# A log-softmax on one core: a row on 4 partitions instead of 8, pieces shifted by their own maximum, stores issued from ScalarE

## The chip, the cores and the metric

Each kernel runs on one core of one Trainium2 chip. The three rounds of experiments ran on three different chips, each with runs of the kernel before beside them. The metric is the device time of one execution in microseconds (us). Every run here was of the fast state, with a granted clock of 1.0, so runs are compared as they are. A ratio is the mean time of one kernel's fast runs over that of the other's fast runs of the same rounds, so it isn't quite the ratio of the medians that are quoted.

## The reference

```python
x: float32 [16, 512, 50000]
shifted = x - max(x, axis=-1)
out = shifted - log(sum(exp(shifted), axis=-1))
```

8192 rows of 50,000 values, each read once and written once: 1638.4 MB each way.

## The kernel before

A row lies on 8 partitions, so a tile is 16 rows, 128 partitions of 6250 columns (25,000 B) and 3.2 MB. There are eight such buffers and 512 tiles. `front` takes the maximum, combines it over the 8 partitions, and sums the exponentials on ScalarE; `back` rewrites the tile in place and stores it. `back` of a tile runs after `front` of the next one. All transfers are issued by SyncE.

```python
G = 8; NBUF = 8; AHEAD = 5

def load(t):
    buf = data.tile([P, W], FP32, name="buf")
    nc.sync.dma_start(out=buf, in_=xt[t])
    ...
def back(t):
    buf = tiles.pop(t)
    nc.vector.tensor_scalar(out=buf, in0=buf, scalar1=shift.pop(t)[:, 0:1],
        scalar2=logs.pop(t), op0=ALU.add, op1=ALU.subtract)
    nc.sync.dma_start(out=ot[t], in_=buf)

for t in range(AHEAD):
    load(t)
for t in range(ntiles + 1):
    if t + AHEAD < ntiles:
        load(t + AHEAD)      # the buffer of tile t + AHEAD - 8
    if t < ntiles:
        front(t)
    if t >= 1:
        back(t - 1)
```

What matters later is the order on SyncE's queue: the load of tile t+5 comes first and waits until the store of tile t-3 has landed, since it takes that buffer; the store of tile t-1 comes behind it.

## Time and profile before

| | before |
|---|---|
| time, median (range) | 7904.87 us (7893.95 to 7924.88) |
| bytes moved, mean rate | 3276.8 MB, 414 GB/s |
| busy: VectorE, ScalarE, TensorE | 70%, 40%, 8% |
| DMA share | 99.9%, one queue |

The prediction shows the page's DMA rows, the chain and the groups. One more view was in the trace and I passed over it: a stretch of the timeline of the kernel before. Its columns are start in us, duration in us, engine, line, operation. "SPq" is SyncE's issuing of a transfer.

```profile
2996.76 3.49 DVE L117 TENSOR_SCALAR buf<-buf,negmax,logsum 128x6250 f32<-128x6250 f32 x1
...
3012.91 0.33 SPq L75 DMA_DIRECT2D buf<-in_x_dram  x1
3012.92 3.50 DVE L117 TENSOR_SCALAR buf<-buf,negmax,logsum 128x6250 f32<-128x6250 f32 x1
...
3013.29 0.43 SPq L121 DMA_DIRECT2D out_dram<-buf  x1
```

The first rewrite ended at 3000.25, yet its store is issued at 3013.29, right after the load at 3012.91. For 13 us a finished tile stood in its buffer because the load ahead of it on the queue was waiting.

### The profile page before, as it was taken

What the parts mean: (1) busy time and instruction counts of PE and PEld (TensorE: products, weight loads), DVE (VectorE), ACT (ScalarE), POOL (GpSimd) and SP (SyncE); (2) the same over time, 40 slices, a digit from 0 to 9 for tenths busy, and PEclk for the clock granted to TensorE, in tenths of its full rate; (3) what the DMA queues carried; (4) which work ended last, traced back from release to release, by engine and by line L of the source; (5) the groups of instructions that cost most, each with busy time, mean ns of one, the idle gap of its engine ahead of it and who ended that gap; (6) DMA issues with size and microseconds to landing.
All of it is one profiled execution on the core that took longest, in us unless ns stands there. A gap on an engine that the chain in (4) does not pass through costs nothing.

```text
span 7908.9 us, 12333 instructions
## 1 busy us (share of the span) xinstructions
PE 600.4 (8%) x2048; PEld 513.0 (6%) x2048; DVE 5566.8 (70%) x3072; ACT 3152.9 (40%) x2561; POOL 1.2 (0%) x7
## 2 busy tenths in 40 slices
PE   0000000000000000000000000000000000000000
PEld 0000000000000000000000000000000000000000
DVE  8777777777777776766666666766666666766665
ACT  4444444444444444333343434333343434333333
POOL 0000000000000000000000000000000000000000
DMA  9999999999999999999999999999999999999999
GB/s 416 426 430 431 431 431 431 431 431 431 431 430 431 429 428 410 410 403 409 409 406 403 404 405 408 407 408 405 409 408 401 406 403 413 408 405 406 406 405 385
DMA packets 147536, 3277.65 MB, mean 414 GB/s; under 512 B 16384, under 2 KB 16384, under 8 KB 16384
## 3 DMA queue, kind: packets, MB, share of 16 engines
q1 hardware_dynamic: 147456, 3276.87, 99.9%
q14 instruction: 64, 0.52, 0.0%
q8 instruction: 16, 0.26, 0.0%
HBM read 1638.40 MB, written 1638.40 MB: 414 GB/s over the span
## 4 chain that ended last, share of the span: by engine, by line
DMA 97%; SPq 1%; DVE 1%; issue 0%; ACT 0%; PE 0%; ACTq 0%
DMA out_dram<-buf 97%; SPq L75 1%; DVE pmax L81 1%; DMA buf<-in_x_dram 0%; DVE buf L117 0%; ACT dump L102 0%; DVE allmax L84 0%; DVE rowmax L86 0%; DVE spread L91 0%; DVE negmax L96 0%; PE rowsum L108 0%; ACT logsum L112 0%; ACTq L102 0%
## 5 line engine op out<-in xcount | busy, mean ns | idle before, releaser
L81 DVE TENSOR_REDUCE pmax<-buf 128x1 f32<-128x6250 f32 x512 | 3411.6, 6663 | 2231.9 <-DMA buf<-in_x_dram 2231.9
L102 ACT ACTIVATE dump<-buf,negmax 128x3125 f32<-128x3125 f32 x1024 | 2937.9, 2869 | 4370.9 <-DVE negmax L96 4354.4
L117 DVE TENSOR_SCALAR buf<-buf,negmax,logsum 128x6250 f32<-128x6250 f32 x512 | 1789.8, 3496 | 4.5 <-ACT logsum L112 3.6
L108 PE MATMUL rowsum<-part,ones 128*128 128x1 f32 x2048 | 600.4, 362 | 7269.8 <-ACT dump L102 7269.8
L108 PEld LDWEIGHTS rowsum<-part,ones 128*128 128x128 f32 x2048 | 513.0, 311 | 7357.1 <-ACT dump L102 7335.3
L112 ACT ACTIVATE logsum<-rowsum 128x1 f32<-128x1 f32 x512 | 87.8, 171 | 345.8 <-PE rowsum L108 345.8
L102 ACT ACTIVATION_READ_ACCUMULATOR dump<-buf,negmax 128x1 f32 x1024 | 190.8, 186 | 0.0
L96 DVE STREAM_TRANSPOSE negmax<-spread 128x32 f32<-128x32 f32 x512 | 108.2, 211 | 17.7
L84 DVE STREAM_TRANSPOSE allmax<-pmax 128x32 f32<-128x32 f32 x512 | 108.2, 211 | 17.5
L86 DVE TENSOR_REDUCE rowmax<-allmax 128x4 f32<-128x32 f32 x512 | 95.3, 186 | 17.8
L91 DVE COPY spread<-rowmax 128x32 f32<-128x32 f32 x512 | 92.9, 181 | 17.8
L67 ACT ACT_TABLE_LOAD x1 | 1.3, 1283 | 0.8 <-PEq L146 0.8
L59 POOL TENSOR_SCALAR_AFFINE_SELECT ones<-ones 128x128 f32<-128x128 f32 x1 | 0.4, 403 | 0.1
L63 POOL TENSOR_SCALAR_AFFINE_SELECT ones<-ones 128x128 f32<-128x128 f32 x1 | 0.4, 398 | 0.1
L57 POOL MEMSET ones<- 128x128 f32 x1 | 0.2, 204 | 0.3 <-POOLq L146 0.3
L146 POOL MEMSET const-bfloat16-1.0<- 128x1 bf16 x1 | 0.1, 102 | 0.0
L146 POOL MEMSET const-uint8-127<- 128x1 uint8 x1 | 0.1, 102 | 0.0
L146 POOL MEMSET const-float32-0.0<- 128x1 f32 x1 | 0.1, 99 | 0.3 <-issue 0.3
L146 POOL MEMSET const-float32-1.0<- 128x1 f32 x1 | 0.1, 99 | 0.0
## 6 DMA issues: line engine op xcount, KB each, us to landing
buf<-in_x_dram SPq DMA_DIRECT2D x512, 3125.0 KB, 23.5
out_dram<-buf SPq DMA_DIRECT2D x512, 3125.0 KB, 30.7
```

What stands on the lines that cost most here:

```text
L59: nc.gpsimd.affine_select(out=ones3, in_=ones3, pattern=[[-G, R], [0, G]], base=0, channel_multiplier=1, compare_op=ALU.is_ge, fill=0.0,)
L67: nc.scalar.preload_act_table_set("natural_log_exp_and_others")
L75: nc.sync.dma_start(out=buf, in_=xt[t])
L81: nc.vector.reduce_max(out=pmax, in_=buf, axis=AX)
L84: nc.vector.transpose(out=allmax, in_=pmax.to_broadcast([P, SQ]))
L86: nc.vector.tensor_reduce(out=rowmax, in_=allmax.rearrange("p (r g) -> p r g", g=G), op=ALU.max, axis=AX, negate=True,)
L91: nc.vector.tensor_copy(out=spread.rearrange("p (r g) -> p r g", g=G), in_=rowmax[:, :, None].to_broadcast([P, SQ // G, G]),)
L96: nc.vector.transpose(out=negmax, in_=spread)
L102: nc.scalar.activation(out=dump, in_=buf[:, j * EXP_C : (j + 1) * EXP_C], func=ACT.Exp, bias=negmax[:, 0:1], scale=1.0, accum_out=part[:, ...
L108: nc.tensor.matmul(rowsum, ones, part[:, j : j + 1], start=j == 0, stop=j == nexp - 1)
L112: nc.scalar.activation(out=logsum, in_=rowsum, func=ACT.Ln)
L117: nc.vector.tensor_scalar(out=buf, in0=buf, scalar1=shift.pop(t)[:, 0:1], scalar2=logs.pop(t), op0=ALU.add, op1=ALU.subtract,)
```

## The change

The intent is fewer, larger tiles: a row on 4 partitions gives 32 rows per tile, 6.4 MB, rows of 50,000 B, four buffers (the same 200,000 B per partition). So that a tile's latency stays short, each piece of 3125 columns is shifted by its own maximum, so that its exponential can run while VectorE reduces the next piece; the four sums are rescaled to the row's maximum at the end. A tile is finished before the next starts. Stores are issued from ScalarE, so they have a queue of their own. The diff, cut to its core:

```diff
-G = 8
+G = 4
-NBUF = 8
-AHEAD = 5
+NBUF = 4
...
-        nc.vector.reduce_max(out=pmax, in_=buf, axis=AX)
...
+        for j in range(nexp):
+            piece = buf[:, j * EXP_C : (j + 1) * EXP_C]
+            nc.vector.tensor_reduce(
+                out=negm[:, j : j + 1], in_=piece, op=ALU.max, axis=AX, negate=True
+            )
+            dump = dump_pool.tile([P, EXP_C], FP32, name="dump")
+            nc.scalar.activation(
+                out=dump, in_=piece, func=ACT.Exp,
+                bias=negm[:, j : j + 1], scale=1.0, accum_out=part[:, j : j + 1],
+            )
...
+        nc.scalar.activation(
+            out=scale, in_=negm, func=ACT.Exp, bias=negmax[:, 0:1], scale=-1.0
+        )
+        nc.vector.tensor_mul(out=scaled, in0=scale, in1=part)
...
-        nc.sync.dma_start(out=ot[t], in_=buf)
+        nc.scalar.dma_start(out=ot[t], in_=buf)
...
+    for t in range(ntiles):
+        compute(t)
+        if t + NBUF < ntiles:
+            load(t + NBUF)
```

More of the change, by code (lines that the diff above doesn't have):

```diff
@@ L69 @@
     tiles = {}
-    shift = {}
-    logs = {}
     def load(t):
@@ L76, in load, with compute @@
         tiles[t] = buf
-    def front(t):
-        buf = tiles[t]
-        pmax = stats.tile([P, 1], FP32, name="pmax")
-        nc.vector.reduce_max(out=pmax, in_=buf, axis=AX)
-        allmax = stats.tile([P, SQ], FP32, name="allmax")
-        nc.vector.transpose(out=allmax, in_=pmax.to_broadcast([P, SQ]))
-        rowmax = stats.tile([P, SQ // G], FP32, name="rowmax")
+    def compute(t):
+        buf = tiles.pop(t)
+        negm = stats.tile([P, nexp], FP32, name="negm")
+        part = stats.tile([P, nexp], FP32, name="part")
+        for j in range(nexp):
[8 more added lines that the diff above has]
+            )
+        negp = stats.tile([P, 1], FP32, name="negp")
+        nc.vector.tensor_reduce(out=negp, in_=negm, op=ALU.min, axis=AX)
+        allneg = stats.tile([P, SQ], FP32, name="allneg")
+        nc.vector.transpose(out=allneg, in_=negp.to_broadcast([P, SQ]))
+        rowneg = stats.tile([P, SQ // G], FP32, name="rowneg")
         nc.vector.tensor_reduce(
-            out=rowmax, in_=allmax.rearrange("p (r g) -> p r g", g=G),
-            op=ALU.max, axis=AX, negate=True,
+            out=rowneg, in_=allneg.rearrange("p (r g) -> p r g", g=G),
+            op=ALU.min, axis=AX,
         )
@@ L92, in front @@
             out=spread.rearrange("p (r g) -> p r g", g=G),
-            in_=rowmax[:, :, None].to_broadcast([P, SQ // G, G]),
+            in_=rowneg[:, :, None].to_broadcast([P, SQ // G, G]),
         )
@@ L96, in front @@
         nc.vector.transpose(out=negmax, in_=spread)
-        shift[t] = negmax
-        part = stats.tile([P, nexp], FP32, name="part")
-        for j in range(nexp):
-            dump = dump_pool.tile([P, EXP_C], FP32, name="dump")
-            nc.scalar.activation(
-                out=dump, in_=buf[:, j * EXP_C : (j + 1) * EXP_C], func=ACT.Exp,
-                bias=negmax[:, 0:1], scale=1.0, accum_out=part[:, j : j + 1],
-            )
+        scale = stats.tile([P, nexp], FP32, name="scale")
+        nc.scalar.activation(
+            out=scale, in_=negm, func=ACT.Exp, bias=negmax[:, 0:1], scale=-1.0
+        )
+        scaled = stats.tile([P, nexp], FP32, name="scaled")
+        nc.vector.tensor_mul(out=scaled, in0=scale, in1=part)
         rowsum = sum_pool.tile([P, 1], FP32, name="rowsum")
@@ L108, in front @@
             nc.tensor.matmul(
-                rowsum, ones, part[:, j : j + 1], start=j == 0, stop=j == nexp - 1
+                rowsum, ones, scaled[:, j : j + 1], start=j == 0, stop=j == nexp - 1
             )
@@ L112, in front @@
         nc.scalar.activation(out=logsum, in_=rowsum, func=ACT.Ln)
-        logs[t] = logsum
-    def back(t):
-        buf = tiles.pop(t)
         nc.vector.tensor_scalar(
-            out=buf, in0=buf, scalar1=shift.pop(t)[:, 0:1], scalar2=logs.pop(t),
+            out=buf, in0=buf, scalar1=negmax[:, 0:1], scalar2=logsum,
             op0=ALU.add, op1=ALU.subtract,
         )
-        nc.sync.dma_start(out=ot[t], in_=buf)
-    for t in range(AHEAD):
+        nc.scalar.dma_start(out=ot[t], in_=buf)
+    for t in range(min(NBUF, ntiles)):
         load(t)
-    for t in range(ntiles + 1):
-        if t + AHEAD < ntiles:
-            load(t + AHEAD)
-        if t < ntiles:
-            front(t)
-        if t >= 1:
-            back(t - 1)
+    for t in range(ntiles):
+        compute(t)
+        if t + NBUF < ntiles:
+            load(t + NBUF)
 _INS = ['x']
```

## The prediction

> **What bounds the kernel now.** I read the page from its DMA rows first, then the chain of waits, then the DMA queue's own waits, then VectorE's groups. The page says this of the transfers and of the chain:
>
> ```profile
> DMA  9999999999999999999999999999999999999999
> GB/s 416 426 430 431 431 431 431 431 431 431 431 430 431 429 428 410 410 403 409 409 406 403 404 405 408 407 408 405 409 408 401 406 403 413 408 405 406 406 405 385
> DMA packets 147536, 3277.65 MB, mean 414 GB/s; under 512 B 16384, under 2 KB 16384, under 8 KB 16384
> q1 hardware_dynamic: 147456, 3276.87, 99.9%
> ...
> HBM read 1638.40 MB, written 1638.40 MB: 414 GB/s over the span
> ...
> DMA 97%; SPq 1%; DVE 1%; issue 0%; ACT 0%; PE 0%; ACTq 0%
> ```
>
> The reader is to see two things. The 16 DMA engines have work all the time (99.9%), on one queue, and the chain that ended last is 97% DMA: the time is bytes over rate, 3276.8 MB at 414 GB/s = 7915 us against a span of 7908.9. And the rate has two regimes: 431 GB/s until about 2.9 ms, then about 406 to the end. A view of the windows 600 to 2600 us and 3000 to 7000 us gives 431 and 407 GB/s at a DMA share of 1.00 in both, so the second regime isn't a lack of queued transfers; the same packets take longer. Per engine 431/16 = 26.94 GB/s is 928 ns for a 25,000 B row, 407/16 is 983 ns: about 55 ns more on the mean. In the packet records of the trace the median stays at 928 ns in the second regime while the slowest tenth takes 1075 ns and more: it is stalls of some packets. What causes them I can't see.
>
> The queue's own waits and the engines' waits:
>
> ```profile
> SPq L75 <- DMA out_dram<-buf: 7333.8, 504, 23.6
> ...
> DVE pmax L81 <- DMA buf<-in_x_dram: 2231.9, 503, 11.1
> ```
>
> The loads wait for a store to free a buffer, in a ring of eight, and VectorE waits for loads 28% of the span. Every compute engine is ahead of the DMA. The groups that I need as prices:
>
> ```profile
> L81 DVE TENSOR_REDUCE pmax<-buf 128x1 f32<-128x6250 f32 x512 | 3411.6, 6663 | 2231.9 <-DMA buf<-in_x_dram 2231.9
> L102 ACT ACTIVATE dump<-buf,negmax 128x3125 f32<-128x3125 f32 x1024 | 2937.9, 2869 | 4370.9 <-DVE negmax L96 4354.4
> L117 DVE TENSOR_SCALAR buf<-buf,negmax,logsum 128x6250 f32<-128x6250 f32 x512 | 1789.8, 3496 | 4.5 <-ACT logsum L112 3.6
> L102 ACT ACTIVATION_READ_ACCUMULATOR dump<-buf,negmax 128x1 f32 x1024 | 190.8, 186 | 0.0
> buf<-in_x_dram SPq DMA_DIRECT2D x512, 3125.0 KB, 23.5
> out_dram<-buf SPq DMA_DIRECT2D x512, 3125.0 KB, 30.7
> ```
>
> A transfer of 3.2 MB alone takes 3.2/414 = 7.7 us, and they land 23.5 and 30.7 us after issue: three to four are queued at any time, some 10 to 13 MB. That is the depth that keeps the engines full.
>
> **What the Trainium skill says.** "DMA: Bandwidth & Descriptors", section "Issuing engines are not separate DMA queues": transfers issued from different engines run on the same 16 DMA engines, and several issuers save only the sequencer's time. Here there is one issuer, and its queue sets 1% of the chain, so there is almost nothing for ScalarE's queue to save. The same page, section "Queues, rings and completion order": each DMA engine takes turns between the queues that have work, packet by packet. With loads on one queue and stores on another they will alternate rather than run in issue order; the kernel before, with one queue, can't show it. The same page, section "Where 436 GB/s comes from": a ceiling of 435 GB/s at the SBUF ports. The first regime, 431, is 1% below it, which agrees, and bounds any gain: 3276.8/435 is 7533 us. "VectorE: DVE Perf Modes", section "The perf-mode tier table": a reduce runs at one element a cycle at most, an fp32 tensor_scalar at two. With the 0.96 GHz and the 151 fixed cycles that the errata section of that page gives for another operation, 6250 elements make (6250+151)/0.96 = 6668 ns; the trace has 6663. So I use that form for the reduce.
>
> **The change part by part.** The bytes are the same, and so is the work per element. What changes is the size of the pieces, the order and the queues.
>
> VectorE per tile (32 rows, 6.4 MB in, 6.4 MB out, 256 tiles). Four reduces of 3125: (3125+151)/0.96 = 3.41 us each, 13.65 us (two of the old were 13.33). The small chain: the old one costs 211+186+181+211 ns; the new has a fifth reduce of 4 columns and a multiply, estimated at 0.19 us each like the small ones: 1.17 us (old, for two tiles: 1.58). The rewrite: 3496 ns less 6250/(2 x 0.96) = 3255 leaves 241 ns fixed, so 12,500/(1.92) + 241 = 6.75 us (old, two: 6.99). Sum 21.6 us per tile, 5520 us in all against 5567: no change.
>
> ScalarE: four exponentials and their accumulator reads, 4 x (2.87+0.19) = 12.2, plus a 4-column exponential and a logarithm at about 0.17 each: 12.6 us per tile, 3220 us in all.
>
> The serial latency is what really moves. Before, tile t-1's rewrite filled the gap in which tile t's exponentials ran. Now a tile is finished before the next starts, so VectorE idles through the tail. The built program's order and waits show that the four reduces wait only for the load and not for ScalarE, so they run back to back: 13.65 + 0.1 of gaps. The exponential (3.06) is shorter than a reduce (3.41), so only the last one sticks out: 0.13 + 3.06, with the 1 us small chain hidden under it; the correcting exponential 0.2; the multiply 0.25; eight matmul passes in a row, from 0.63 us for one column's two (seen from accumulator read to logarithm) plus three times 0.5 to 0.59 for the others, 2.2; the logarithm 0.25; the rewrite 6.75 + 0.1. Sum 26.7 us per tile. The DMA needs 12.8 MB per tile: 29.7 us at 431, 31.5 at 407. So compute stays hidden, with only 3 to 5 us to spare where it had 9 of 31.
>
> Buffers: the same 200,000 B per partition. A buffer's cycle is four tile periods, about 124 us at 414 GB/s. Less 26.7 of compute and about 4 of issue and receipt, 93 us remain for two transfers, that is three transfers of 6.4 MB in flight on the mean, some 19 MB. As long as the latency is below the period, at most one buffer is in compute and the other three are in transfer or waiting to be computed, so the engines always have a transfer queued; only when the latency passes the period (29.7 us at 431, 31.5 at 407) do loaded buffers pile up in front of VectorE. So no starvation, but the cliff is 3 us away.
>
> The DMA's own rate. (a) Packets of 50,000 B in place of 25,000. If the 9 ns by which 928 exceeds 25,000 B at 435/16 GB/s (919) are paid per packet, the new ones take 1847 ns, 433 GB/s: 0.5% of the first 2.95 ms, 15 us. (b) The stalls of the second regime, 55 ns of 983 on the mean, over 4950 us, cost 277 us. If each packet risks one stall, half the packets means half the stalls, 138 us saved; if it goes with bytes or addresses, nothing. I give the first one chance in three: 45 us. (c) Two queues that alternate: I put zero, with a wide spread. (d) The end: after the last load 26.7 us of compute and 15 us of store, of which the previous store fills 15; about 12 us with the DMA idle, against a few before: +10 us. Sum 7904 - 15 - 45 + 10 = 7854 us.
>
> **The rivals.** First, latency becomes the bound: the tail or the reduces are longer than I say, DVE reaches 30 to 32 us per tile, and VectorE's own chain sets 256 x 31 = 7940 us or 256 x 33 = 8450. For it: no overlap between tiles, the 3 us of slack. Against it: every term but the matmuls' is a measured duration. Second, alternating reads and writes change the rate of the DMA engines. If they go at 431 to 433 throughout, the time is about 7600; if they fall to 395 throughout, 8300. For either there is only the second regime, which shows that the rate isn't fixed. Against: in the kernel before loads and stores are already in flight together, since the engines run apart from each other by up to a transfer. Third, nothing: the second regime is fixed by addresses or elapsed time, and the result is 7890 to 7915. This is the likeliest single outcome.
>
> **Range and chances.** The middle is 7854. Losing a second regime that depends on packets or on queue order is worth up to 4%; a slightly worse mix of reads and writes, or latency at the edge, costs 2%. So 7620 to 8050 in 8 of 10. Faster by over 2% is below 7746 and needs more than half of the second regime's loss to vanish: 0.25. Slower by over 2% is above 8062 and needs a rate below 406 all along, or the latency bound: 0.17. The rest, 0.58.
>
> **What would show it right or wrong.** Right: DMA at 9 in all slices, packets halved to about 65,500 of 50,000 B plus small ones, reduces of 3.41 us and a rewrite of 6.75 us; the first reduce of most tiles waits for its load, 3 to 5 us; VectorE waits about 5 us per tile for the logarithm and the correction; the first slices at 431 to 433. The slices after 3 ms tell (b) and (c): 406 means that packets and queues don't matter, 418 that stalls are halved, 431 that they are gone. Wrong: reduces that wait for no load (the latency bound), DMA slices below 9, or a rate in the first slices under 425, which would put the blame on the alternating queues.

## The result, and the profile after

The changed kernel takes 7637.72 us (median of 4 runs, 7616.13 to 7721.55) against 7904.87: ratio 0.9679, 95% interval 0.9601 to 0.9757, faster. The profile is of the slowest of the four, 7721.55.

These are the rows of the page of the changed kernel that answer to those of before: transfers, chain, groups and issues.

```profile
DMA  9999999999999999999999999999999999999998
GB/s 416 433 433 434 431 434 433 432 432 432 431 431 431 412 411 420 407 415 412 411 412 407 410 427 431 431 432 432 428 431 431 430 432 428 427 429 426 431 430 385
DMA packets 73806, 3277.60 MB, mean 425 GB/s; under 512 B 8192, under 2 KB 8192, under 8 KB 8192
q1 hardware_dynamic: 36864, 1638.42, 50.7%
q10 hardware_dynamic: 36864, 1638.42, 49.1%
...
another core or an unknown queue 95%; DMA 1%; DVE 1%; SPq 1%; ACT 0%; issue 0%; PE 0%; ACTq 0%
...
L86 ACT ACTIVATE dump<-buf,negm 128x3125 f32<-128x3125 f32 x1024 | 2937.3, 2868 | 3987.3 <-DVE negm L82 3985.6
L82 DVE TENSOR_REDUCE negm<-buf 128x1 f32<-128x3125 f32 x1024 | 3418.4, 3401 | 1104.4 <-DMA buf<-in_x_dram 1104.4
L122 DVE TENSOR_SCALAR buf<-buf,negmax,logsum 128x12500 f32<-128x12500 f32 x256 | 1738.3, 6790 | 553.7 <-ACT logsum L121 553.7
...
buf<-in_x_dram SPq DMA_DIRECT2D x256, 6250.0 KB, 41.1
out_dram<-buf ACTq DMA_DIRECT2D x256, 6250.0 KB, 52.6
```

Still the DMA engines are busy all the time. What changed is the rate: 426 to 434 GB/s in the middle slices, but for a slow stretch of 407 to 420 in slices 14 to 23, after which it recovers. In the kernel before the slow stretch began at 2.9 ms and stayed to the end. The chain view is of little use here: "an unknown queue 95%" means that it couldn't follow the second DMA queue back.

The timeline of the changed kernel, in the same columns, shows the store:

```profile
3016.41 6.79 DVE L122 TENSOR_SCALAR buf<-buf,negmax,logsum 128x12500 f32<-128x12500 f32 x1 [2.17 <-ACT logsum L121]
3023.23 0.34 ACTq L126 DMA_DIRECT2D out_dram<-buf  x1
```

The rewrite ends at 3023.20 and the store is issued at 3023.23, with nothing ahead of it.

From the landing times follows how much is in flight, that is issued and not yet landed: time to landing times the rate of that direction, half of the total. Before: (23.5 + 30.7) us x 207 MB/ms = 11.2 MB. After: (41.1 + 52.6) x 212 = 19.9 MB, out of the same buffer space.

### The profile page after: what moved, and what is told of

The parts are those of the page before. It is cut to its first block, busy times and chain, and to the rows that moved or that the text cites. A ratio compares the mean times of both kernels' runs of the same rounds, so it can differ in the third digit from the quotient of the medians.

```text
span 7719.8 us, 12071 instructions
## 1 busy us (share of the span) xinstructions
PE 477.8 (6%) x2048; PEld 455.9 (6%) x2048; DVE 5440.7 (70%) x2816; ACT 3156.7 (41%) x2561; POOL 1.4 (0%) x7
## 4 chain that ended last, share of the span: by engine, by line
another core or an unknown queue 95%; DMA 1%; DVE 1%; SPq 1%; ACT 0%; issue 0%; PE 0%; ACTq 0%
SPq L72 1%; DVE negm L82 1%; DMA buf<-in_x_dram 1%; DMA out_dram<-buf 1%; DVE buf L122 0%; ACT dump L86 0%; PE rowsum L117 0%; ACT scale L110 0%; ACT logsum L121 0%; DVE scaled L114 0%; ACTq L86 0%
## 5 line engine op out<-in xcount | busy, mean ns | idle before, releaser
L86 ACT ACTIVATE dump<-buf,negm 128x3125 f32<-128x3125 f32 x1024 | 2937.3, 2868 | 3987.3 <-DVE negm L82 3985.6
L82 DVE TENSOR_REDUCE negm<-buf 128x1 f32<-128x3125 f32 x1024 | 3418.4, 3401 | 1104.4 <-DMA buf<-in_x_dram 1104.4
L122 DVE TENSOR_SCALAR buf<-buf,negmax,logsum 128x12500 f32<-128x12500 f32 x256 | 1738.3, 6790 | 553.7 <-ACT logsum L121 553.7
L117 PE MATMUL rowsum<-scaled,ones 128*128 128x1 f32 x2048 | 477.8, 355 | 7218.0 <-DVE scaled L114 7218.0
L117 PEld LDWEIGHTS rowsum<-scaled,ones 128*128 128x128 f32 x2048 | 455.9, 327 | 7239.8 <-DVE scaled L114 7203.9
L86 ACT ACTIVATION_READ_ACCUMULATOR dump<-buf,negm 128x1 f32 x1024 | 190.9, 186 | 0.0
L110 ACT ACTIVATE scale<-negm,negmax 128x4 f32<-128x4 f32 x256 | 72.1, 282 | 0.0
L106 DVE STREAM_TRANSPOSE negmax<-spread 128x32 f32<-128x32 f32 x256 | 54.1, 211 | 8.9
L94 DVE STREAM_TRANSPOSE allneg<-negp 128x32 f32<-128x32 f32 x256 | 54.1, 211 | 8.9
L96 DVE TENSOR_REDUCE rowneg<-allneg 128x8 f32<-128x32 f32 x256 | 47.6, 186 | 8.9
## 6 DMA issues: line engine op xcount, KB each, us to landing
buf<-in_x_dram SPq DMA_DIRECT2D x256, 6250.0 KB, 41.1
out_dram<-buf ACTq DMA_DIRECT2D x256, 6250.0 KB, 52.6
```

What stands on the lines that cost most here:

```text
L82: nc.vector.tensor_reduce(out=negm[:, j : j + 1], in_=piece, op=ALU.max, axis=AX, negate=True)
L86: nc.scalar.activation(out=dump, in_=piece, func=ACT.Exp, bias=negm[:, j : j + 1], scale=1.0, accum_out=part[:, j : j + 1],)
L94: nc.vector.transpose(out=allneg, in_=negp.to_broadcast([P, SQ]))
L96: nc.vector.tensor_reduce(out=rowneg, in_=allneg.rearrange("p (r g) -> p r g", g=G), op=ALU.min, axis=AX,)
L106: nc.vector.transpose(out=negmax, in_=spread)
L110: nc.scalar.activation(out=scale, in_=negm, func=ACT.Exp, bias=negmax[:, 0:1], scale=-1.0)
```

## The experiments

The question is why the rate falls, and which part of the change prevents it. The first rivals were the packet size (a stall per packet, as in the prediction), the queues, and addresses or elapsed time. Ten kernels ran; all gave correct results. The times of before in the same calls lay between 7838.65 and 7938.71 us, medians 7895 to 7907.

### First round: one part alone

**Two queues, nothing else.** The kernel before, with

```diff
-        nc.sync.dma_start(out=ot[t], in_=buf)
+        nc.scalar.dma_start(out=ot[t], in_=buf)
```

> The kernel before with one edit: stores issued from ScalarE, so loads and stores lie on two queues (packets still 25,000 B, eight buffers). If the two queues are what spares the stalls, the time falls to 7620 to 7720 us and the slices after 3 ms show 425 to 431 GB/s. If the packet size is, it stays at 7890 to 7930 with about 406 after 3 ms.

Measured: 7614.08 us (7613.96 to 7616.15), ratio 0.9639 with interval 0.9622 to 0.9656. That is a little under the lowest time expected. This one line gives all of the gain. Its rate row:

```profile
GB/s 425 433 432 431 432 432 432 432 432 432 432 432 432 432 432 432 432 432 432 432 432 432 432 432 432 432 433 432 432 432 432 432 432 432 432 432 432 432 433 380
```

**One queue, all else of the change.** The changed kernel, with

```diff
-        nc.scalar.dma_start(out=ot[t], in_=buf)
+        nc.sync.dma_start(out=ot[t], in_=buf)
...
-        if t + NBUF < ntiles:
-            load(t + NBUF)
+        if t >= 1 and t + NBUF - 1 < ntiles:
+            load(t + NBUF - 1)
```

> The changed kernel with all transfers on one queue (stores issued from SyncE, each load issued one tile later so that it doesn't block the store behind it). If packets of 50,000 B are what spares the stalls, the time stays at 7610 to 7720 us. If the two queues are, a second regime of about 406 to 410 GB/s comes back and the time is 7830 to 7910.

Measured: 7601.05 us (7600.88 to 7601.22), ratio 0.9622. There is no slow stretch:

```profile
GB/s 425 432 433 433 433 432 433 433 433 434 432 433 433 432 433 434 432 432 433 433 432 433 434 433 432 433 433 433 433 433 433 433 433 432 433 433 433 432 433 379
```

So the two queues aren't needed either. By the expectation's wording this spoke for the packets, but then the two-queue kernel with 25,000 B packets should have stayed slow. That the store isn't held back here has another reason: the load that stands ahead of it waits for a store issued a whole tile of 30 us earlier. The queue's own waits show it: SyncE spends 2834 us waiting for the rewrite, where before it spent 73.

```profile
SPq L72 <- DMA out_dram<-buf: 4550.9, 251, 19.9
SPq L126 <- DVE buf L122: 2834.0, 256, 41.2
```

**Half-size packets.** The changed kernel, each load and each store cut in two by columns:

```diff
-        nc.sync.dma_start(out=buf, in_=xt[t])
+        for h in range(2):
+            s = slice(h * W // 2, (h + 1) * W // 2)
+            nc.sync.dma_start(out=buf[:, s], in_=xt[t][:, s])
# and the store likewise
```

> The changed kernel with each load and each store cut into two transfers of 6250 columns, so packets of 25,000 B on two queues, tiles and buffers as they are. Fixed cost alone (928 against 1847/2 = 923.5 ns for 25,000 B) makes it 0.5% slower: 7650 to 7680. If stalls are per packet, it goes to 7750 to 7850; if the queues are what matters, it stays at 7640 to 7720.

Measured: 7634.62 us (7613.94 to 7651.05), the changed kernel's own time, and a little under the expectation. Packets of 25,000 B don't stall more: the packet theory falls. (Its profile, like its place in the table below, is of the fastest of the four runs, 7613.94.)

**Tiles in reverse order.** The kernel before with `xt[ntiles - 1 - t]` and `ot[ntiles - 1 - t]`.

> The kernel before with the tiles taken from the last to the first. If the slow regime belongs to addresses, the slow 62% come first: about 406 GB/s in the first 25 slices and 431 in the last 15, time about 7905. If it belongs to elapsed time or to how the engines drift, 431 comes first again and the slow regime begins at some later slice that need not be the same.

Measured: 7919.95 us, ratio 1.0025. The rate starts at 430 and falls at about 2.6 ms:

```profile
GB/s 418 430 429 431 430 431 430 431 431 431 430 430 431 421 409 405 408 407 409 404 412 407 406 404 402 402 410 407 408 405 404 411 406 402 406 410 403 402 407 386
```

Not addresses, then.

### A new theory: the engines drift apart until the fast ones run dry

Each transfer is carried by 16 DMA engines, and the trace has the 16 times at which they report a transfer's end. From these records I worked out, for each transfer, the time from the first engine's report to the last one's, and took medians over stretches of 400 us:

```
median us from first to last engine, stretches beginning at
ms                0.0  0.4  0.8  1.2  1.6  2.0  2.4  2.8  3.2  3.6  4.0  5.2  6.0  7.2
before            2.2  5.0  7.3  8.2 10.3 11.6 11.5 12.6 13.3 13.2 13.5 13.4 13.2 13.3
e4_reversed       2.6  4.9  7.4  9.0 11.2 11.6 12.1 13.2 13.3 13.3 13.2 13.2 13.2 13.4
e1_two_queues     1.4  2.8  4.1  5.3  7.0  8.3 10.0 11.1 12.4 14.0 15.3 19.4 21.8 22.3
e2_one_queue      3.1  5.2  6.1  7.4  8.4 10.0 11.3 12.4 13.9 15.0 16.0 20.7 22.9 26.7
```

The engines drift apart steadily. In the kernel before the spread stops at 13.3 us, and that is when the rate falls. The order on the queue gives a reason for the stop: when the store of tile t-3 has landed on all engines, two transfers are still queued behind it (the load of t+4 and the store of t-2), 14.9 us at 431 GB/s. Less about 1.6 us for reporting and issuing (an estimate: 14.9 less the 13.3 seen), that is as far ahead as a fast engine can be before its queue is empty. In the two fast variants the spread passes 20 us without a loss.

The packet records show how little of the loss is empty queues. Two us after a load is issued, 15.1 of the 16 engines have a packet under way in the slow regime (3.5 to 7.3 ms) and 16 in the fast one (0.6 to 2.6 ms), so some fast engines do run empty there. But the DMA share of 3 to 7 ms is still 0.999. Nearly all of the loss is packets that take longer: 982 ns on the mean in place of 932, with the median at 928 in both.

### Second round: depth and drift

**One number.** The kernel before with

```diff
-AHEAD = 5
+AHEAD = 4
```

> The kernel before with one number changed: loads run 4 tiles ahead in place of 5, so a load waits for the store of four tiles back in place of three. One queue, packets of 25,000 B, eight buffers. Theory 'depth': the 16 DMA engines drift apart (in the kernel before the time between the first and the last engine's end of a transfer grows from 2 us to 13.3 us, stays there, and there the rate falls); 13.3 us is what is still queued when the awaited store lands (two transfers, 14.9 us, less 1.6). With four transfers queued (29.7 us) the drift never gets there in 7600 us, so no slow regime: 7605 to 7640 us, 431 GB/s in all slices. Rival 'packets or queues': 25,000 B on one queue is what stalls, so 7890 to 7930 with 406 GB/s.

Measured: 7676.01 us (7656.95 to 7682.67), ratio 0.9727 with interval 0.9661 to 0.9794. Loading less far ahead makes it faster, since a load now waits for an older store and more is queued behind that one. The size was missed by 36 us or more; the rate row tells where a part of it lies:

```profile
GB/s 416 428 430 431 431 431 431 431 431 431 431 430 431 431 431 431 431 431 431 431 431 430 431 431 431 431 431 430 431 431 430 431 430 430 429 430 426 412 410 361
```

The slow regime comes after all, in the last three slices (the last one also holds the end of the run). The spread reaches 26.3 to 26.6 us from 5.2 ms on and 28.8 at 7.2 ms, against 29.7 less 1.6 = 28.1. So the same limit is met, later. And it isn't the spread alone: at 5.0 ms, with the spread already at 25, three of the 16 engines were within 2 us of the first and nothing was lost; at 7.0 ms it was eleven. In the kernel before it was 5 at 2.0 ms, 12.6 at 3.2 ms, 14 at 5.0 ms (means over 20 transfers). In both kernels the rate fell when most engines had caught up with the limit and started their transfers together.

**Three stops.** The kernel before, 5 ahead, where after every 128 tiles the first load waits for the last store on all engines:

```diff
+    SEG = 128
+    for s in range(0, ntiles, SEG):
+        if s:
+            nc.gpsimd.memset(last[0][:, 0:1], 0.0)   # waits for the last store
...
+        if first:
+            nc.gpsimd.memset(buf[:, 0:1], 0.0)       # the load into buf waits for this
```

> The kernel before, 5 ahead, with three stops: after every 128 tiles (about 1.9 ms) the next load waits until the last store has landed on all engines. Theory 'depth': the drift starts from zero at each stop and doesn't reach 13.3 us, so 431 GB/s all along but for a stop of some 15 to 25 us each: 7650 to 7700. Rival 'elapsed time, heat or a neighbour': slow from 2.9 ms on as before, plus the stops: 7940 to 7980.

Measured: 7686.36 us (7681.67 to 7688.85), ratio 0.9743. Depth, queue, packets and tiles are those of the kernel before; only the drift is wiped out three times, and the slow regime doesn't come:

```profile
GB/s 416 426 430 431 431 431 431 430 431 408 419 426 430 429 430 431 431 431 431 409 418 424 429 430 431 431 431 431 431 410 418 423 430 430 430 431 430 431 431 409
```

The dips at slices 10, 20 and 30 are the stops. The spread grows to 11.4, falls to 3.2 and grows again, and never reaches 13. This excludes elapsed time as such. By the landing times it has only 11.0 MB in flight, no more than the kernel before: that depth is enough as long as the engines haven't drifted up to the limit.

**No depth.** The kernel before with `AHEAD = 6`.

> The kernel before with loads 6 tiles ahead: a load waits for the store of two tiles back, and when that lands nothing is queued behind it. Theory 'depth': slow from the start, each pair of transfers costs the 14.9 us plus 1.5 to 3 us of issue and landing: 8400 to 9200 us. Rival 'packets or queues': no dependence on this number, 7890 to 7930.

Measured: 9721.44 us, ratio 1.2324, worse than expected: 19.0 us per pair of transfers.

```profile
GB/s 356 339 340 338 334 336 329 341 333 340 333 336 335 341 336 337 336 337 341 334 339 335 336 341 337 335 336 337 341 337 333 333 338 335 333 336 326 339 338 354
```

The spread is 0.9 to 1.4 us: all engines move in step. The loss has two parts. The DMA share is 0.88, so the engines stand empty for 12% of the time, 2.3 us of the 19.0; and a packet takes 1042 ns on the mean in place of 928, which turns the 14.9 us of two transfers into 16.7. Here the stalls can be dated. By the packet records, a packet that starts in the first us after a load is issued takes 880 ns longer than the usual 928, one that starts 8 us after it 665 ns longer, and one from 3 to 6 or from 11 to 16 us after it nothing. These are the moments at which the engines begin a load or a store together. In the late part of the kernel before the stalls lie at the same places, 75 to 133 ns at 1 to 3 us and 87 to 256 ns at 7 to 10 us, and none after 11 us; between 3 and 7 us they are 22 to 48 ns.

**Three buffers.** The changed kernel with `NBUF = 3`.

> The changed kernel with three 50 KB buffers in place of four, two queues and 50,000 B packets kept. Theory 'depth': some 13 MB in flight in place of 20 and fast engines run dry, so the rate falls to about 400 to 412 within the first quarter: 7850 to 8300 us. Rival 'packets or queues': three buffers suffice on the mean (89 us cycle less 31), so 7620 to 7720.

Measured: 7917.61 us, ratio 1.0037. Two queues and 50,000 B packets, with less in flight, and all of the gain is gone. The engines don't have to drift first: the spread is 1.5 to 4.6 us throughout, with 13 to 15 of them within 2 us of the first:

```profile
GB/s 407 423 408 423 407 397 419 411 416 409 414 408 413 402 421 421 423 416 412 419 420 420 424 410 410 402 411 411 411 408 421 418 402 424 412 415 411 415 412 396
```

The runs, by MB in flight (landing times as above):

| kernel | queues, packet | in flight, MB | rate, GB/s | time, us |
|---|---|---|---|---|
| AHEAD = 6 | 1, 25,000 B | 5.0 | 337 throughout | 9721 |
| three stops | 1, 25,000 B | 11.0 | 431, with three dips | 7686 |
| before | 1, 25,000 B | 11.2 | 431, then 406 from 2.9 ms | 7905 |
| changed, G = 8 (third round) | 2, 25,000 B | 12.2 | 426 to 432 | 7678 |
| changed, three buffers | 2, 50,000 B | 13.7 | 397 to 424 throughout | 7918 |
| changed, half packets | 2, 25,000 B | 16.9 | 429 to 433 | 7635 |
| AHEAD = 4 | 1, 25,000 B | 17.3 | 431, then 411 from 7.1 ms | 7676 |
| two queues | 2, 25,000 B | 19.2 | 432 | 7614 |
| changed | 2, 50,000 B | 19.9 | 432, with a slow stretch in the profiled run | 7638 |
| changed, one queue | 1, 50,000 B | 19.9 | 433 | 7601 |

Neither the number of queues nor the packet size divides this table. The depth does so only roughly: the five kernels with 16.9 MB and more took 7676 us or less, but inside that group it orders nothing, and two kernels with 11.0 and 12.2 MB held the rate. One of these has its drift reset; the other, with G = 8, is bound by the latency of its tiles, and its stores land after 19.2 us. So MB in flight is a mark and not the cause. What the runs with one queue show is how much is queued at the moment a load is released, against how far the engines have drifted.

### Third round: what the other parts are for

**Without the pieces.** The changed kernel with one maximum over the whole 12,500 columns, then the four exponentials, no rescaling:

```diff
-        for j in range(nexp):
-            nc.vector.tensor_reduce(out=negm[:, j : j + 1], in_=piece, ...)
+        nc.vector.tensor_reduce(out=negp, in_=buf, op=ALU.max, axis=AX, negate=True)
```

> The changed kernel with the maximum of the whole row first and the exponentials after it, as the kernel before has them; tiles, buffers and queues as changed. What the pieces are for, by the prediction's terms: reduce of 12,500 13.2 us, chain 1.1, four exponentials 12.3, matmuls and logarithm 1.1, rewrite 6.8, together 34.5 us per tile against the 29.7 us of the DMA, so 256 x 34.5 = 8830 us with the DMA share well below 1. If the pieces don't matter it stays at 7640 to 7720.

Measured: 8700.05 us, ratio 1.1011. The timeline of one tile carries it:

```profile
2996.48 13.17 DVE L79 TENSOR_REDUCE negp<-buf 128x1 f32<-128x12500 f32 x1
...
3010.66 2.87 ACT L98 ACTIVATE dump<-buf,negmax 128x3125 f32<-128x3125 f32 x1 [20.92 <-DVE negmax L93]
...
3023.61 6.79 DVE L109 TENSOR_SCALAR buf<-buf,negmax,logsum 128x12500 f32<-128x12500 f32 x1 [13.02 <-ACT logsum L108]
3030.31 13.17 DVE L79 TENSOR_REDUCE negp<-buf 128x1 f32<-128x12500 f32 x1
```

From reduce to reduce it is 33.83 us (34.5 expected; most matmuls hide under the exponentials), and VectorE waits 13 us for the logarithm, and no longer for loads. With a tile finished before the next begins, the pieces are what keeps the latency under the DMA's 29.7 us.

**A row on 8 partitions.** The changed kernel with `G = 8`, `NBUF = 8`.

> The changed kernel with a row on 8 partitions and eight 25 KB buffers, pieces and queues kept, so two pieces per tile and no overlap between tiles. By the measured terms a tile takes 6.7 (two reduces) + 3.2 (last exponential sticking out) + 0.5 (correction and multiply) + 1.2 (matmuls, logarithm) + 3.5 (rewrite) = 15.1 us against 14.9 of the DMA, so the latency bound is just reached: 7720 to 7800 us. If only the depth in flight matters, it is as the two-queue version of the kernel before: 7610 to 7640.

Measured: 7678.00 us, ratio 0.9717, between the two expectations: the tiles follow at 14.94 us, and 512 x 14.94 = 7649. The latency bound is just touched, less hard than I had said. VectorE waits for a load only once in the run, at the start, and the rate holds:

```profile
GB/s 425 432 432 432 432 432 432 432 432 432 432 432 430 432 430 430 427 429 428 430 428 430 427 430 429 427 428 429 428 429 428 426 430 429 428 428 429 428 429 330
```

## Why the prediction was right or wrong

The time, 7637.72, lies in the range and near its lower end. The middle, 7854, missed most of the gain. "Faster by over 2%" had been given one chance in four and "nothing" had been called the likeliest outcome, so that the range held owes more to its width than to its reasons.

**The bound, and the bytes over the rate: right.** The DMA is busy in all slices and the time is bytes over rate. The 7533 us, an estimate from the 435 GB/s that "DMA: Bandwidth & Descriptors" gives, wasn't reached: the fastest run took 7601. The section that it comes from, "Where 436 GB/s comes from", says that for transfers between HBM and SBUF the HBM side, about 358 GB/s, is what binds. The prediction left this out; 431 to 433 GB/s was measured here, on one core, and the measurement decides. VectorE is busy 5441 us (5520 said), ScalarE 3157 (3220).

**The latency of a tile: right, and a little generous.** From the first reduce at 2997.43 to the end of the rewrite at 3023.20 it is 25.8 us, 26.7 said. The four reduces take 13.35 in a row (13.75 with gaps said), the rewrite 6.79 (6.75). The waits came as said: 1104.4/256 = 4.3 us for a load per tile (3 to 5), 554/256 = 2.2 for the logarithm and 2.2 for the correction (about 5 together). So the first rival, latency as the bound, was rightly put aside; the run without pieces shows where its cliff is.

**Term (a), 0.5% from larger packets: right for a packet, not shown for a kernel.** In the packet records a 50,000 B row takes 1847 ns, as said. In whole kernels, 7601 with one queue and 50,000 B lies 13 us below 7614 with two queues and 25,000 B, but these two differ in more than the packets; and halving the packets of the changed kernel made it no slower (7635 against 7638).

**Term (b) and (c): the step that failed.** The prediction says that "the second regime isn't a lack of queued transfers; the same packets take longer". It was drawn from the DMA share of 1.00. The stops and the one number show that it was a lack of queued transfers, measured against the drift: the fast engines of the 16 had run into the end of what was queued, and had bunched. "The same packets take longer" was read rightly (982 ns in place of 932); what didn't follow is that enough was queued. The share hardly shows it, since the longer packets count as busy. With the cause misjudged, (b) became one chance in three of half the stalls (45 us) and (c) zero, where 7898 (the kernel before in the same call) to 7614 in the two-queue run, which changes no packet, is 284 us. "Almost nothing for ScalarE's queue to save", drawn from SyncE's 1% of the chain, failed with it: that 1% is the time of issuing and doesn't contain the 13 us for which a finished store stood behind a waiting load. The second rival, "431 to 433 throughout, about 7600", came nearest, but for the slow stretch of the profiled run, and not by alternation of reads and writes: one queue does it as well.

**The buffers: the right number, the wrong use of it.** "Three transfers of 6.4 MB in flight on the mean, some 19 MB" was met at 19.9. I asked only whether that keeps the queues from being empty, and didn't set it against the 10 to 13 MB that I had just read off the kernel before.

**Term (d), the end: not told apart.** The last slice is 385 GB/s in both profiles.

**What stays open.** It is open why the engines drift (at 2.0 to 2.4 ms the last report comes 0.8 to 3.5 us after the one before it in four drifting kernels, as if one engine alone were the slowest, but the records don't name it). It is open, too, what collides when they start together, and when: in two kernels with two queues and 25,000 B packets 12 engines on the mean stood within 2 us of the first (two queues from 0.6 to 2.2 ms, G = 8 from 3.6 to 7.3 ms) and a packet took 928 and 936 ns, so that bunching without an empty queue costs little or nothing there.

In the late part of the kernel before I could follow the last engine back through 237 of its transfers: about half take 7424 ns, eight clean packets, and about a quarter more than 8307, so even an engine that never runs dry is slowed. That the others' start slows it is argued from the places of the stalls and not shown.

Last, it is open why the changed kernel falls into its slow stretch, whether its other runs have one (they weren't profiled), and why it leaves it. At 2.6 and 3.2 ms the spread of its stores is 29 us (of its loads 18) with 12 engines within 2 us of the first, as the theory asks; at 5 ms it is 26 us with 9. I made no run on its recovery.

The fastest kernel of all is the changed one with a single queue and the load one tile later: 7601.05 us, ratio 0.9622, against a bytes-over-rate time of 3276.8/433 = 7568.

## What to carry to other kernels

In a streaming kernel with a full DMA, look at what is queued at the moment a load is released, not only at whether the DMA is busy: a queue issued in order that makes a load wait for a recent store holds finished stores back behind it, and fewer tiles of lookahead, or the stores on another queue, were worth 3% to 4% here. A rate that fell in the middle of the run for no reason in the program was the sign of it, and a few stops that let all engines meet were a cheap test. The pieces, which shorten a tile's latency, paid because without them it was 33.8 us against the 29.7 us of the tile's transfers.

## What the Trainium skill lacked or had wrong

- "DMA: Bandwidth & Descriptors", section "Rules for kernel authors", says that spreading transfers over several issuers for bandwidth doesn't help and saves only sequencer time. Moving the stores to ScalarE, one line, gave 0.9639 of the time here. The rate's ceiling isn't raised (432 against 431), but an issuer's in-order waits are removed: stores had stood ready for 13 us.
- The same page has nothing on how far the 16 engines drift apart over a kernel (from 3 to 27 us between the first and the last in the 7601 us of the one-queue variant), or that they lose rate when they bunch at the end of what is queued: 406 in place of 431 GB/s with two transfers of 3.2 MB queued behind the awaited store, 411 and only from 7.1 ms with four, 337 from the start with none.
